# Storing the first tile's output by one transfer of eight rows a partition instead of two of four

## The chip, the cores and the metric

One core of a Trainium2 chip runs the kernel. The metric is the device time of one execution in microseconds (us); a kernel's time is the median of its runs. "Span" is the time from the first to the last instruction in the profiled execution, some 1.3 us less than the device time.

Data moves between HBM (the chip's main memory) and the core's on-chip buffers, which have 128 partitions, by sixteen DMA engines. A load reads HBM, a store writes it. A packet is one data record of the trace: here the rows of one partition in one transfer. A transfer has landed when all engines have reported it (16 updates of its semaphore in the trace). ScalarE computes GELU, VectorE the product, and SyncE only waits and issues transfers.

## The reference

The input has 32 x 512 rows of 2048 float32 values. The first half of each row goes through GELU and is multiplied by the second half:

```
x1, x2 = x[..., :1024], x[..., 1024:]
out = 0.5 * x1 * (1 + erf(x1 / sqrt(2))) * x2
```

So 134.2 MB are read and 67.1 MB written.

## The kernel before

The 16384 rows are cut into 16 tiles of 128 partitions x 8 rows. Tile i uses input buffer i % 2 (64 KB a partition) and output buffer i % 2 (32 KB a partition). SyncE issues all loads and the last three stores (queue q1); ScalarE issues the other stores (queue q10). Tile 0 and tile 15 are computed in three steps, the others in two.

```python
load(0, slice(0, 4), first)
load(0, slice(4, 8), loaded[0])
load(1, slice(0, 8), loaded[1])
...
for i in range(n_tiles):
    k = i % 2
    last = i == n_tiles - 1
    pieces = i == 0 or last
    steps = ((0, 2), (2, 4), (4, 8)) if pieces else ((0, 5), (5, 8))
    if i >= 2:
        nc.scalar.wait_ge(stored[k], n[stored[k].name])   # the output buffer is free
    for lo, hi in steps:
        ...  # ScalarE: GELU of these rows; VectorE: product, counted in mul_done
        if pieces and hi % 4 == 0:
            if last:
                store(nc.sync, i, slice(hi - 4, hi), tail_stored)
            else:
                store(nc.scalar, i, slice(hi - 4, hi), stored[k])
    if not pieces:
        if i == n_tiles - 2:
            store(nc.sync, i, slice(0, R), tail_stored)
        else:
            store(nc.scalar, i, slice(0, R), stored[k])
    if i + 2 < n_tiles:
        nc.sync.wait_ge(mul_done, n[mul_done.name])       # the input buffer is free
        load(i + 2, slice(0, R), loaded[k])
```

Two waits tie the tiles together: tile i's compute needs store i-2 to have landed, and load i+2 is issued only after tile i's compute.

## Time and profile before

| | before |
|---|---|
| median of the runs | 469.6 us (469.56 to 471.63) |
| span of the profiled run | 468.1 us |
| packets of q1 and q10, share of 16 engines' span | 70.5% + 29.1% |
| bytes of HBM over the span | 201.3 MB, 430 GB/s |
| VectorE, ScalarE busy | 30%, 25% |

The lines of the profile, and how they are read, stand in the prediction.

### The profile page before, as it was taken

The page shows a single profiled execution, that of the slowest core. Times are in us where ns is not written, and L with a number is a line of the kernel's source. Part 1 is how long each engine was busy: PE and PEld are TensorE (multiplying, and loading weights), DVE is VectorE, ACT ScalarE, POOL GpSimd, SP SyncE. Part 2 cuts the span into 40 slices and gives each one's busy share as a digit, 9 for nine tenths or more (in the row PEclk, how much of TensorE's full clock was granted, in tenths as well). Part 3 has the DMA queues.
Part 4 walks back from the last instruction along what each step waited for, and adds up shares of the span by engine and source line. Part 5 has one row for each costly group of instructions (what it writes and reads, how often), then busy time and mean ns, then how long its engine had stood idle before and what let it go on. Part 6 is the DMA issues. An engine that isn't in the chain of part 4 may idle for free.

```text
span 468.1 us, 174 instructions
## 1 busy us (share of the span) xinstructions
DVE 140.5 (30%) x34; ACT 115.5 (25%) x35; POOL 0.2 (0%) x4
## 2 busy tenths in 40 slices
DVE  0330514207052060511606116060150702507043
ACT  1320606032060410604106050050500506014060
POOL 0000000000000000000000000000000000000000
DMA  8999899999999999999999999999999999999998
GB/s 358 448 448 442 375 423 496 414 403 445 417 482 403 420 431 493 403 403 448 470 426 403 442 409 493 403 403 448 493 403 403 448 442 454 404 428 423 493 395 367
DMA packets 5041, 201.34 MB, mean 430 GB/s; under 512 B 560, under 2 KB 560, under 8 KB 560
## 3 DMA queue, kind: packets, MB, share of 16 engines
q1 hardware_dynamic: 2880, 142.61, 70.5%
q10 hardware_dynamic: 2160, 58.72, 29.1%
q14 instruction: 1, 0.01, 0.0%
HBM read 134.22 MB, written 67.11 MB: 430 GB/s over the span
## 4 chain that ended last, share of the span: by engine, by line
DMA 76%; DVE 14%; ACT 8%; ACTq 0%; SPq 0%; issue 0%
DMA out_dram<-o_tile 66%; DVE o_tile L87 14%; DMA x_tile<-in_x_dram 10%; ACT o_tile L79 8%; ACTq L110 0%; SPq L47 0%; SPq L63 0%; SPq L58 0%
## 5 line engine op out<-in xcount | busy, mean ns | idle before, releaser
L87 DVE TENSOR_TENSOR o_tile<-o_tile,x_tile 128x5120 f32<-128x5120 f32 (+3 forms) x34 | 140.5, 4170 | 320.2 <-ACT o_tile L79 320.2
L79 ACT ACTIVATE o_tile<-x_tile 128x5120 f32<-128x5120 f32 (+3 forms) x34 | 114.3, 3407 | 337.4 <-DMA out_dram<-o_tile 301.9
L79 ACT ACT_TABLE_LOAD x1 | 1.3, 1283 | 3.3 <-PEq L63 3.3
L133 POOL MEMSET const-bfloat16-1.0<- 128x1 bf16 x1 | 0.1, 102 | 0.0
L133 POOL MEMSET const-uint8-127<- 128x1 uint8 x1 | 0.1, 102 | 0.0
L133 POOL MEMSET const-float32-1.0<- 128x1 f32 x1 | 0.1, 99 | 0.0
L133 POOL MEMSET const-float32-0.0<- 128x1 f32 x1 | 0.1, 98 | 0.2 <-issue 0.2
## 6 DMA issues: line engine op xcount, KB each, us to landing
out_dram<-o_tile ACTq DMA_DIRECT2D x13, 4096.0 KB, 44.7
x_tile<-in_x_dram SPq DMA_DIRECT2D x2, 4096.0 KB, 16.7
out_dram<-o_tile ACTq DMA_DIRECT2D x2, 2048.0 KB, 34.4
out_dram<-o_tile SPq DMA_DIRECT2D x1, 4096.0 KB, 25.1
out_dram<-o_tile SPq DMA_DIRECT2D x2, 2048.0 KB, 7.6
x_tile<-in_x_dram SPq DMA_DIRECT2D x15, 44.5
```

Source lines behind the costliest of these rows:

```text
L79: nc.scalar.activation(out=o_bufs[k][:, rows, :], in_=x_bufs[k][:, rows, :half], func=GELU),
L87: nc.vector.tensor_mul(out=o_bufs[k][:, rows, :], in0=o_bufs[k][:, rows, :], in1=x_bufs[k][:, rows, half:],),
L133: nc = _bacc.Bacc("TRN2", target_bir_lowering=False, num_devices=1)
```

## The change

The intent is fewer, larger transfers: one store of 4 MiB in place of two of 2 MiB. The price is that nothing of tile 0's output can leave before all of tile 0 is computed. Tile 15 keeps its two stores.

```diff
-            if pieces and hi % 4 == 0:
-                if last:
-                    store(nc.sync, i, slice(hi - 4, hi), tail_stored)
-                else:
-                    store(nc.scalar, i, slice(hi - 4, hi), stored[k])
-        if not pieces:
+            if last and hi % 4 == 0:
+                store(nc.sync, i, slice(hi - 4, hi), tail_stored)
+        if not last:
             if i == n_tiles - 2:
                 store(nc.sync, i, slice(0, R), tail_stored)
             else:
```

## The prediction

> **What bounds the kernel now.** I read the page from its head (busy shares, then the DMA row of the slices), then the chain of waits in order of time, then the timeline of the first tiles, and last the windows, cut at the moments that the timeline gave.
>
> ```profile
> span 468.1 us, 174 instructions
> DVE 140.5 (30%) x34; ACT 115.5 (25%) x35; POOL 0.2 (0%) x4
> ...
> DMA  8999899999999999999999999999999999999998
> ...
> DMA packets 5041, 201.34 MB, mean 430 GB/s; under 512 B 560, under 2 KB 560, under 8 KB 560
> q1 hardware_dynamic: 2880, 142.61, 70.5%
> q10 hardware_dynamic: 2160, 58.72, 29.1%
> ```
>
> The two computing engines work under a third of the span. The DMA row is 9 or just below from end to end, and the packets of q1 (SyncE's queue: all loads and the last three stores) and q10 (ScalarE's queue: all other stores) take 70.5 + 29.1 = 99.6% of sixteen engines' span, which is 466.2 of 468.1 us. So the transfers leave about 2 us unfilled in the whole program. The time is their sum, plus the start.
>
> ```profile
> 12.99 3.71 ACT L79 ACTIVATE o_tile<-x_tile 128x2048 f32<-128x2048 f32 x2 [8.43 <-DMA x_tile<-in_x_dram]
> 19.45 0.38 ACTq L53 DMA_DIRECT2D out_dram<-o_tile  x1
> 22.70 3.62 ACT L79 ACTIVATE o_tile<-x_tile 128x4096 f32<-128x4096 f32 x1 [6.00 <-DMA x_tile<-in_x_dram]
> 30.81 0.36 ACTq L53 DMA_DIRECT2D out_dram<-o_tile  x1
> 47.30 7.12 ACT L79 ACTIVATE o_tile<-x_tile 128x5120 f32<-128x5120 f32 x2 [20.99 <-DMA x_tile<-in_x_dram]
> 60.60 0.36 ACTq L53 DMA_DIRECT2D out_dram<-o_tile  x1
> 71.68 7.12 ACT L79 ACTIVATE o_tile<-x_tile 128x5120 f32<-128x5120 f32 x2 [17.25 <-DMA out_dram<-o_tile]
> ...
> 100.68 7.12 ACT L79 ACTIVATE o_tile<-x_tile 128x5120 f32<-128x5120 f32 x2 [21.88 <-DMA out_dram<-o_tile]
> ```
>
> This is the start, from the timeline. Each half of tile 0's load takes 9.7 us (12.99 to 22.70), the first half's store goes out at 19.45, the second's at 30.81. Tile 1 can start at 47.30, tile 2 at 71.68, tile 3 at 100.68, and from there each tile follows 29.0 us after the one before. ScalarE's wait ends with a store's landing, but that is only a name: 8 MiB of load and 4 MiB of store go through in each 29.0 us.
>
> ```profile
> 22.30:46.92 24.62, 4.43 (x1) 3.62 (x1) 0.00 (x0) 1.00 0.99 426
> 46.92:71.60 24.68, 8.76 (x2) 7.12 (x2) 0.00 (x0) 1.00 0.99 428
> 100.68:129.68 29.00, 8.76 (x2) 7.12 (x2) 0.00 (x0) 1.00 1.00 434
> ```
>
> The windows give, in the last two columns, the DMA share and the rate. The two stretches in which tile 0's stores drain (load 1 with the first, load 2 with the second) run at 426 and 428 GB/s, a steady period at 434. That small gap is all that the change can reach in the middle of the stream.
>
> **What the Trainium skill says.** "DMA: Bandwidth & Descriptors", section "Queues, rings and completion order", says each DMA engine goes round-robin between the queues it has work for, one packet at a time. The trace agrees: its packet records alternate between q1 and q10, and a steady period holds, on each engine, eight load packets of 64 KB (2.418 us) and eight store packets of 32 KB (1.213 us): 8 x 3.631 = 29.05 against 29.0 us. The same page, "Where 436 GB/s comes from", puts the ceiling of the sixteen ports at 435.2 GB/s and says that for transfers to or from HBM a lower limit of some 358 binds. The steady 434 shows that here the ceiling, not the lower limit, is what counts. "Perfetto Trace Analysis", section "DMA Optimizations", says splitting may let part of a transfer start sooner, and ties the gain to DMA engines that are generally idle. Here they are not idle, so I expect little loss from undoing the split.
>
> **The change part by part.** Tile 0 still loads in two halves and computes in three steps. Removed: the store issued at 19.45 and that queue entry (0.38 us of ScalarE's sequencer, in a wait of 6.00 us). Added: nothing. Altered: the one store at 30.81 carries eight rows a partition. The order of the other engines' instructions is unchanged.
>
> Packets: tile 0's stores were 16 packets of 16 KB on each engine at 0.611 us = 9.78 us. They become 8 of 32 KB at 1.213 = 9.70 us. Saved: 0.07 us, on the path that sets the end, since the stream is full.
>
> Order: with 16 KB store packets, load 1 and load 2 each took 80% of the bytes while they ran (64 of 80 KB a round). In the changed kernel load 1 runs alone from 22.3 us until the store's first packet. A load issued at 0.94 had its first packet at 1.95, so I take 1.0 us from issue to eligibility: 31.8 us, in the middle of a change of packets. Five load packets then go alone (choosing that the next one is already committed): 22.3 + 5 x 2.42 = 34.4. The other three alternate with 32 KB stores: 3 x 3.63 = 10.9, so load 1's data ends at 45.3; its completion passes behind one more store packet (1.21) and takes 0.4 us as now: tile 1 starts near 46.9 (if only four go alone, 48.1). By then four of store 0's eight packets are out. Load 2 then alternates all along, with the other four of store 0 and then with store 1 (issued at 46.9 + 13.3 = 60.2, in time to follow store 0, which ends near 61.0). Load 2 ends at 45.3 + 8 x 3.63 = 74.3 and tile 2 starts near 75.9, against 71.68 now, 4.2 us later.
>
> That is not lost time: during it three packets of store 1 have gone (3.6 us of stream) which before were still to come. Every later tile keeps the same offset at 29.0 us a tile, with ScalarE released by its load, not by a store. At the end the stores in the ScalarE queue run out three packets before load 15 does, and its last packets go alone. Count the whole stream: from 22.3 us, 15 loads x 8 x 2.418 = 290.2, plus 14 stores x 8 x 1.213 = 135.9, gives 448.4 for the end of the last load, so tile 15 starts at 448.8; before it started at 448.97. The tail is as now: store 14 takes 8 x 1.213 = 9.7, the two halves of the last store 4.9 each, and end of data to landing 0.4: 448.4 + 9.7 + 9.8 + 0.4 = 468.3, which is the span before (468.1) to within the rounding of these terms.
>
> Left over is the rate of the two slow stretches. They hold 40 packets' worth of 32 KB on each engine in 24.62 + 24.68 = 49.3 us; at 29.0/24 = 1.208 us each they would hold it in 48.3. If the changed kernel's stream runs at the steady rate there, it gains 1.0 us (the 0.07 is part of it). The records show single 64 KB packets of 2.5 to 2.8 us there beside 2.418; whether the 16 KB stores cause them or the start of a transfer, the trace does not say, so I take half: 0.5 us. Sum: 469.6 - 0.5 = 469.1 us.
>
> **The rivals.** First, that stores which start 11 us later leave the DMA engines dry. Against it: at 19.45 q1 still holds the rest of load 0 and all 8 MiB of load 1, and the stretch where loads ran alone moved 4 MiB in 9.7 us, 432 GB/s. To lose 2% (9.4 us) the engines would have to stand still for nearly the whole 11 us. It would make 471 to 480.
>
> Second, that the later landing of store 0 becomes a wait for tile 2, which writes the same output buffer. By my count store 0 lands about 62 to 64, load 2 at 75.9, so the wait is covered by 12 us. If it were not, tile 2 would shift, but the next load is already queued and the stream runs on: no change in time.
>
> Third, that the offset of 4.2 us reaches the end: tile 15 starts at 453 instead of 448.8, and its compute up to the last store (448.97 to 460.67 = 11.7 us) is exposed. For it: that is what a fixed period would give. Against it: the stores in ScalarE's queue are finite, and the three packets sent early are missing at the end. It would make 472 to 473.
>
> Fourth, that the slow stretches are fully the small packets' doing: 468.6.
>
> **Range and chances.** 469.1 us; 8 in 10 between 468.3 and 470.4, the upper side for the run-to-run spread (one of three runs before was 471.63) and for a part of the third rival. All rivals but the worst form of the first lie within 2% of 469.6 (460.2 to 479.0). Faster by over 2%: 0.01; within: 0.98; slower: 0.01.
>
> **What would show it.** In the changed profile: DMA packet shares again summing to about 99.6%; tile 1 starting near 47 to 48 and tile 2 near 76 to 77; ScalarE's waits put down to the loads of x_tile instead of stores; stores landing about 34 us after issue instead of 44.7 (issued 13.3 after the tile's start, first packet 18 after, last 47 after); tile 15 starting within half a microsecond of 448.97; the span within 1 us of 468.1. A DMA slice at 7 or less between 19 and 35 us, or tile 15 after 450, would prove me wrong.

## The result, and the profile after

The changed kernel took 470.74 us (median of 6 runs, 470.02 to 471.29) against 469.6 us, a ratio of 1.0016 with a 95% interval of 0.9998 to 1.0035. Ratios here are the mean time of one kernel's fast runs over that of the other's in the same rounds, so not quite the ratio of the medians quoted. Executions over 1.5% slower than the fastest of the same kernel are left out of the means. In a second set of five runs, told below, the ratio was 1.0029 (1.0015 to 1.0043). So there is a small real loss, about a quarter of a per cent, where a small gain was predicted; the median lies 0.3 us above the stated range (the ratio times 469.6 is 470.35, just inside it). The first interval is wide because one of the six runs before took 471.63 us; it has no profile, and none of the 16 later runs of that kernel is above 469.76.

From the page of the changed kernel: the span, the DMA row, and the two queues.

```profile
span 468.7 us, 173 instructions
...
DMA  8998989999999999999999999999999999989998
...
q1 hardware_dynamic: 2880, 142.61, 70.6%
q10 hardware_dynamic: 2016, 58.72, 29.0%
```

The shares sum to 99.6% again, and q10 has 144 records fewer (2160 before): 128 store packets and the 16 completions of the second transfer. Nothing ran dry. Next the timeline of the start (start, duration, engine and line; in brackets how long the engine had been idle and what ended it).

```profile
30.78 0.38 ACTq L53 DMA_DIRECT2D out_dram<-o_tile  x1
46.85 7.12 ACT L79 ACTIVATE o_tile<-x_tile 128x5120 f32<-128x5120 f32 x2 [20.56 <-DMA x_tile<-in_x_dram]
76.00 7.12 ACT L79 ACTIVATE o_tile<-x_tile 128x5120 f32<-128x5120 f32 x2 [22.03 <-DMA x_tile<-in_x_dram]
104.92 7.12 ACT L79 ACTIVATE o_tile<-x_tile 128x5120 f32<-128x5120 f32 x2 [21.80 <-DMA x_tile<-in_x_dram]
...
449.40 7.21 ACT L79 ACTIVATE o_tile<-x_tile 128x2048 f32<-128x2048 f32 x3 [17.98 <-DMA x_tile<-in_x_dram]
```

Tile 1 starts 0.45 us earlier than before, tile 2 then 4.3 us later (76.00 against 71.68), and every further tile keeps that offset until the last, which starts at 449.40 against 448.97. ScalarE is now released by loads where it was released by stores: 337.8 us of its waits are put down to x_tile, none to out_dram. The whole middle of the program has moved by 4 us and the end has not.

The windows show where the stream was not full speed (last column GB/s):

```profile
22.30:45.22 22.92, 4.42 (x1) 3.62 (x1) 0.00 (x0) 1.00 0.95 392
45.20:74.20 29.00, 8.76 (x2) 7.12 (x2) 0.00 (x0) 1.00 1.00 434
```

A window counts a packet whole where it starts, and that misleads here: on most engines load 1's first packet starts just before 22.3 us and is left out, so 392 is too low. With each packet spread over its own time, load 1's stretch ran at 414 GB/s (428 before) and load 2's at 434 (431 before). The packet records of the trace were also taken apart by engine: for each of the 16 DMA engines the chain of its packets (the records name no engine; a packet belongs to the one whose last packet ended at that moment), and by how much single packets exceeded their usual time (2.418 us for 64 KB, 1.213 for 32 KB, 0.611 for 16 KB).

```
packets held up, mean of 16 engines        before      after
first store joins the load stream          0.34 us     1.08 us   (load packets starting 20 to 47 us)
second half store beside load 2            0.11 us     -         (47 to 75 us)
last packet of the slowest engine ends     467.73      468.28 us
```

Before, the excess is spread over several packets of 0.06 to 0.40 us. After, each engine has exactly one, the sixth load packet of load 1 (start near 34 us), which takes 3.43 to 3.59 us instead of 2.42; the first store packet follows it at 37.4 to 38.0 us. More held up: 1.08 - 0.45 = 0.63 us; saved by larger packets: 0.07 us. Together 0.56 us, and the last packet ends 0.55 us later. This accounts for the two profiled spans (468.7 against 468.1), but not for the runs near 471.3.

### The profile page after: what moved, and what is told of

Read it like the earlier page. It is cut to its first block, busy times and chain, and to the rows that moved or that the text cites. A ratio compares the mean times of both kernels' runs of the same rounds, so it can differ in the third digit from the quotient of the medians.

```text
span 468.7 us, 173 instructions
## 1 busy us (share of the span) xinstructions
DVE 140.5 (30%) x34; ACT 115.5 (25%) x35; POOL 0.2 (0%) x4
## 4 chain that ended last, share of the span: by engine, by line
DMA 76%; DVE 14%; ACT 8%; ACTq 0%; issue 0%; SPq 0%
DMA x_tile<-in_x_dram 76%; DVE o_tile L87 14%; ACT o_tile L79 8%; ACTq L107 0%; SPq L47 0%; ACTq L77 0%; SPq L63 0%; SPq L58 0%
## 5 line engine op out<-in xcount | busy, mean ns | idle before, releaser
L79 ACT ACTIVATE o_tile<-x_tile 128x5120 f32<-128x5120 f32 (+3 forms) x34 | 114.3, 3407 | 337.8 <-DMA x_tile<-in_x_dram 337.8
## 6 DMA issues: line engine op xcount, KB each, us to landing
out_dram<-o_tile ACTq DMA_DIRECT2D x14, 4096.0 KB, 33.6
```

What stands on the lines that cost most here:

```text
L79: nc.scalar.activation(out=o_bufs[k][:, rows, :], in_=x_bufs[k][:, rows, :half], func=GELU),
```

## The experiments

Twelve kernels ran, in three groups, each group compared with runs of the kernel before (medians 469.50, 469.50 and 469.57 us).

**Again.** The changed kernel unaltered.

> The changed kernel, unaltered, for a second profile and a tighter interval. Theory of the full stream (the time is the sum of the packets plus what single packets are held up): 470.0 to 471.3 us, the sixth packet of load 1 again held up by about 1.1 us when the first store enters the stream. Rival, that the 1.1 us between the medians is chance: a ratio to the kernel before of 1.000 and a range that covers 469.6.

Measured: 471.32 us (five runs: 470.19, 470.23, 471.32, 471.52, 471.53), ratio 1.0029 (1.0015 to 1.0043). The nine runs of the kernel before beside it lay within 469.41 to 469.58. The sixth packet is held up again, and the rival (chance) falls. The profiled execution was one of the three longer ones, with a span of 470.0 us, and its chains show why:

```
again, engine chains: load packets before the first store, that store's start, packets held up, last end
15 engines    22    37.40 to 37.89 us    0.86 to 1.53 us in all          468.08 to 468.40 us
 1 engine     21    35.13 us             0.80 + 1.83, 2.62 us in all     469.62 us
```

One engine of sixteen took the store one packet earlier than the others and was held up twice. In these records each engine moves eight of a transfer's 128 packets, and a tile starts only after the last engine's (tile 1 at 49.41 us, against 46.85 in the first profile), so this one engine's end sets the time: 469.62 - 468.28 = 1.34 us, and the span is 1.3 us longer than in the first profile. Why an engine takes this turn in some executions is open; the first store's first packet falls close to a change of packets, and the neighbours differ by up to half a microsecond there.

**Two late halves.** Small packets without the early start.

```diff
+            elif i == 0:
+                store(nc.scalar, i, slice(0, 4), stored[k])
+                store(nc.scalar, i, slice(4, 8), stored[k])
```

> Tile 0's output again as two transfers of four rows, but both issued when all of tile 0 is done: small packets without the early start. Full stream with round-robin by packets: 16 packets of 16 KB an engine take 16 rounds beside 64 KB load packets, store 0 lands near 86 us, tile 2 must wait for it, load 4 is issued near 100 instead of 89, and the stream may run dry for 1 to 3 us: about 471.5 us (470 to 473.5). Rival, that only bytes count: 469.6 to 470.7. Rival, that the small packets themselves are the better form: below 469.6.

Measured: 472.11 us, ratio 1.0054 (1.0019 to 1.0088), the four runs at 469.97, 470.37, 473.85 and 473.97. The profiled one was of 470.37: tile 2 starts at 84.04, released by the store (predicted about 86), and the next two tiles close up until the 29 us rhythm is there again. No dry stretch is seen in that execution. What the two runs near 473.9 lose can't be said without a profile of one. In these four runs, small packets without the early start are not better than one large transfer.

**Finer and earlier.** One transfer after each of tile 0's three steps.

```diff
             if last and hi % 4 == 0:
                 store(nc.sync, i, slice(hi - 4, hi), tail_stored)
-        if not last:
+            elif i == 0:
+                store(nc.scalar, i, slice(lo, hi), stored[k])
+        if not pieces:
```

> The other direction: tile 0's output in three transfers, each issued as soon as its step is done (two, two and four rows). Round-robin by packets: 24 store packets an engine instead of 16 or 8, so store 0 needs 24 rounds beside the 64 KB loads and lands near 90 us, although it begins earlier; tile 2 waits for it, load 4 is issued near 103 us, loads and stores in flight are used up near 100 us and the stream is dry for 3 to 5 us: 473 us (471 to 475). Rival, that an earlier start of stores helps or is hidden: 469.6 or less.

Measured: 474.33 us, ratio 1.0102 (1.0088 to 1.0116). The timeline of tiles 1, 2 and 3:

```profile
45.59 7.12 ACT L79 ACTIVATE o_tile<-x_tile 128x5120 f32<-128x5120 f32 x2 [18.20 <-DMA x_tile<-in_x_dram]
88.95 7.12 ACT L79 ACTIVATE o_tile<-x_tile 128x5120 f32<-128x5120 f32 x2 [36.24 <-DMA out_dram<-o_tile]
102.71 7.12 ACT L79 ACTIVATE o_tile<-x_tile 128x5120 f32<-128x5120 f32 x2 [6.63 <-DVE o_tile L87]
```

Tile 2 waits 36 us for store 0, whose first piece went out at 17.36. A window from 98 to 105 us shows what this costs:

```profile
70.00:98.00 28.00, 4.54 (x1) 7.12 (x2) 0.00 (x0) 1.00 0.99 429
98.00:105.00 7.00, 4.22 (x2) 2.29 (x1) 0.00 (x0) 1.00 0.84 286
```

The rate falls to 286 GB/s, and the records have a gap of 2.5 to 3.9 us on every engine before load 4's first packet. The stores began earliest of all kernels, and yet tile 2 was released 4.9 us later than by the 16 packets of the two late halves (84.04), because 24 small packets need 24 turns beside packets of 64 KB. That the turns are counted in packets, not in bytes, is what this run shows.

**Later.** The store of tile 0 only after tile 1.

```diff
-            else:
+            elif i > 0:
+                if i == 1:
+                    store(nc.scalar, 0, slice(0, R), stored[0])
+                store(nc.scalar, i, slice(0, R), stored[k])
```

> More of the change: the one transfer of tile 0 is issued only when tile 1 is done (near 55 us instead of 31). Full stream by my count: loads 1 and 2 run alone to about 58 us, store 0 then needs 8 rounds of 3.63 us and lands near 88 to 90, tile 2 waits for it, load 4 is issued near 103 and the stream is dry for some 5 us: 475 us (472 to 478). Rival, that the order of a stream never matters: 470 to 471. Rival, that each us of a later store costs a us: over 490.

Measured: 474.73 us, ratio 1.0122 (1.0105 to 1.0139). The timeline again:

```profile
42.14 7.12 ACT L79 ACTIVATE o_tile<-x_tile 128x5120 f32<-128x5120 f32 x2 [15.75 <-DMA x_tile<-in_x_dram]
89.18 7.12 ACT L79 ACTIVATE o_tile<-x_tile 128x5120 f32<-128x5120 f32 x2 [39.91 <-DMA out_dram<-o_tile]
102.94 7.12 ACT L79 ACTIVATE o_tile<-x_tile 128x5120 f32<-128x5120 f32 x2 [6.64 <-DVE o_tile L87]
```

Tile 2 waited until 89.18 (expected 88 to 90), and the engines stood still for 2.5 to 3.8 us near 104. (The profiled execution was the slowest of the four, 476.86 us: one engine ended at 475.1, the others at 473.8 to 473.9. The other three lay within 474.65 to 474.74.) Putting the store off by 11 us cost a quarter of a per cent; by 36 us, 1.2%. So both rivals fall: a store's delay is not paid one for one, and the order of the stream does matter once the output buffer comes free after the loads in flight are used up.

**A used queue.** The first of tile 0's rows in each partition is loaded through ScalarE's queue (lines joined in this cut and the next).

```diff
-        load(0, slice(0, 4), first)
+        counted(nc.scalar.dma_start(out=x_bufs[0][:, 0:1, :], in_=x_t[0][:, 0:1, :]), first, 16)
+        load(0, slice(1, 4), first)
```

> The changed kernel, but the first of the four rows of load 0's first half is loaded through ScalarE's queue, so that this queue has been used before the first store. Theory A, that the 1.05 us hold-up of one load packet at the first store is the first use of the second queue: the hold-up goes to under 0.3 us and the time to about 469.8 (469.4 to 470.3). Theory B, that a store packet entering a stream of loads alone holds up the load packet ahead of it by about its own length (1.2 us for 32 KB, 0.6 for 16 KB): hold-up still 0.9 to 1.2 us, 470.0 to 471.5 us, in two groups. Theory C, that issuing store 0 and load 2 within 0.02 us of each other is the cause: as B.

Measured: 470.81 us (470.02 to 471.69), ratio 1.0025 (1.0013 to 1.0038). The packet near 34 us is held up by 0.96 to 1.32 us on fifteen engines; one engine was early again, held up by 0.99 and 1.53 us, in a profiled run of 471.69 us. Theory A, the first use of the queue, falls. The row moved was a load, though: that the first store of a program is special, whatever its queue did before, is not excluded by this run.

**Two issues apart.** An additional VectorE product delays load 2's issue.

```diff
+        if i == 0:
+            counted(nc.vector.tensor_mul(out=o_bufs[1][:, 0:4, :],
+                in0=x_bufs[0][:, 0:4, :half], in1=x_bufs[0][:, 0:4, half:]), mul_done, 1)
+            nc.scalar.wait_ge(mul_done, n[mul_done.name])
```

> The changed kernel, but an additional product on VectorE (4096 elements a partition, 4.4 us, written to the other output buffer before its use and overwritten later) delays the issue of load 2 from 30.8 to about 35.2 us; store 0 is still issued at 30.8, and load 1 runs beyond 41 us, so no supply is lost. Theory C (two issues at once): hold-up of the sixth packet under 0.4 us and about 469.8 us. Theories A (first use of the queue) and B (the store packet's length): hold-up still near 1.05 us, 470.0 to 471.5.

Measured: 470.56 us (469.97 to 471.24), ratio 1.0023 (1.0009 to 1.0036). Load 2 was issued at 35.27, the store at 30.94, and on fifteen of the engines the packet that starts near 34 us was held up by 0.68 to 1.43 us, with a smaller hold-up of the one before on most; the sixteenth again took the store early. So two issues at the same moment are not the cause. But 35.27 still lies inside the held-up packet (34 to 38 us), so this run doesn't exclude that the issue of load 2 plays a part.

**No load in flight, after and before.** Load 1 is issued when tile 0 is done, in each of the two kernels.

```diff
-        load(1, slice(0, 8), loaded[1])
 ...
             nc.sync.wait_ge(mul_done, n[mul_done.name])
+            if i == 0:
+                load(1, slice(0, 8), loaded[1])
```

> The changed kernel without load 1 in flight behind load 0: load 1 is issued only when all of tile 0 is computed. Now the DMA engines are dry from 22.3 us to the first packets after 30.8, about 9.5 us. Full stream: 469.6 + 9.5 = 479 us (477.5 to 481). Rival, that other stages hide it: under 475.

> The kernel before (two stores of four rows) without load 1 in flight, as in the run before this one. The first store, issued at 19.5 us, can now fill 4.9 us of the dry stretch (2 MiB at 16 packets of 0.61 us a half). Full stream: 4.3 to 5 us less than the changed kernel without the load: 474.5 us (473 to 476), a difference of about 1% that the split earns where the engines are dry. Rival, that the split is worth nothing anywhere: no difference.

Measured: 481.90 us with one store (above the expected range) and 476.03 with two (at its upper edge). The split that was worth 1.1 to 1.8 us in the tuned kernel (the differences of the medians in the two sets) is worth 5.9 us here. First the window of the one-store form, then those of the two-store form:

```profile
22.30:31.70 9.40, 4.42 (x1) 3.62 (x1) 0.00 (x0) 1.00 0.00 0
```

```profile
22.30:27.30 5.00, 0.35 (x1) 3.62 (x1) 0.00 (x0) 1.00 0.98 419
27.30:32.30 5.00, 4.08 (x1) 0.00 (x0) 0.00 (x0) 1.00 0.00 0
```

With one store, nothing moves for 9.4 us; with two, the first half moves at 419 GB/s in the first five of these. The expectation counted only the gap: the one-store form lost 12.4 us, not 9.5. The records show the rest as held-up packets: 0.96 to 1.84 us on nearly every engine in the first load packet after the dry stretch, just ahead of the store, smaller ones near 79 us on most, and one engine with 3.7 us in all that ended at 480.6, the others by 479.4. The two-store form also has 0.29 to 1.40 us in that first load packet, so this is not the doing of the one large store alone. The late engine accounts for more than a microsecond of the profiled run: without it the last packets of the two profiled kernels would be 5.1 us apart (479.4 against 474.3), near the 4.3 to 5 us expected.

**The last store's queue, after and before.** Store 14 from ScalarE's queue, in each of the two kernels.

```diff
             if i == n_tiles - 2:
-                store(nc.sync, i, slice(0, R), tail_stored)
+                store(nc.scalar, i, slice(0, R), tail_stored)
```

> The changed kernel with store 14 issued from ScalarE's queue instead of SyncE's. My account of the end says that the offset of some 4 us is given back only because the last stores of ScalarE's queue run out before load 15 does, and store 14 waits behind load 15. Then here store 14 takes every second turn beside load 15's last three packets: load 15 lands 3.6 us or more later, tile 15 starts near 453.5 instead of 449.4 to 450.6, its compute is exposed, and the time is about 473.5 us (472 to 475). Rival, that only the sum of bytes counts: 470 to 471.5.

> The same edit on the kernel before. There load 15 and store 13 end together, so store 14 starts at the same moment on either queue: tile 15 starts at 449 us and the time is unchanged, 469.6 us (469.2 to 470.4). Rival, that the queue of store 14 costs by itself: as much loss as in the changed kernel.

Measured: 473.44 us after the change (ratio 1.0077, 1.0059 to 1.0095), 469.52 us before it (ratio 0.9999, 0.9983 to 1.0015). Tile 15's first line, in the changed kernel with this edit, then in the kernel before with it:

```profile
454.09 7.21 ACT L79 ACTIVATE o_tile<-x_tile 128x2048 f32<-128x2048 f32 x3 [21.52 <-DMA x_tile<-in_x_dram]
```

```profile
449.05 7.21 ACT L79 ACTIVATE o_tile<-x_tile 128x2048 f32<-128x2048 f32 x3 [21.86 <-DMA out_dram<-o_tile]
```

The window in which tile 15 of the former is computed:

```profile
454.00:461.50 7.50, 4.66 (x3) 7.21 (x3) 0.00 (x0) 1.00 0.58 251
```

The offset reaches the end here, tile 15 starts at 454.09, and the stream runs empty under its compute: the records have gaps of 1.7 to 3.5 us on every engine near 461.5. In the kernel before, whose load 15 and store 13 end together, the same edit costs nothing. So the offset of 4 us is real work put off, and what gives it back in the changed kernel is that store 14 queues behind load 15.

**Six rows and two.** Tile 0's output as two transfers of six and two rows, issued together (the edit of the two late halves with other bounds).

> The changed kernel with tile 0's output as two transfers issued together, of six rows (24 KB packets) and two rows (8 KB). Theory B, the hold-up of the load packet at the first store grows with the store packet: between the 0.4 us mean of 16 KB and the 1.05 to 1.3 of 32 KB, about 0.75 to 0.9 us. Rival, a fixed hold-up: 1.0 to 1.3. The time, as with two late halves (16 rounds): 470 to 474.5 us.

Measured: runs at 470.08, 470.11 and 472.72 us, median 470.11 (a fourth, at 479.78, is left out; with it the median is 471.42), ratio 1.0040 (1.0002 to 1.0078). The packet near 34 us is held up by 0.47 to 0.80 us, 0.65 on average. This is between 16 and 32 KB, a little under the range expected.

**Smaller load packets.** Load 1 as two transfers of four rows.

```diff
-        load(1, slice(0, 8), loaded[1])
+        load(1, slice(0, 4), loaded[1])
+        load(1, slice(4, 8), loaded[1])
```

> The changed kernel with load 1 as two transfers of four rows (load packets of 32 KB instead of 64 when the first store arrives). Theory B, the hold-up belongs to the store packet: 1.0 to 1.3 us still. Theory D, it belongs to the load packet: near half, 0.5 to 0.65 us. The time: 469.6 to 471.5 us, since the stream stays full.

Measured: 470.36 us, four runs within 470.19 to 470.45, ratio 1.0017 (1.0001 to 1.0033). The hold-up is spread over two packets, 0.93 us an engine in all, so it is not halved with the load packet, against theory D; it is a little below B's range. Two engines took the store a packet early, but here a packet is 1.2 us, and they ended at 468.4 to 468.5, the others at 467.7 to 468.2. The runs near 471.3 are absent, which fits the account of the early engine, in four runs.

The hold-up at the first store, over the runs (mean an engine, summed over the load packets up to 47 us, of "later" over 50 to 70):

```
store packet   kernel                                  held up
16 KB          before (first store at 19.5 us)         0.34 us (0.21 at the first store, 0.10 at the second)
16 KB          two late halves                         0.94 us (0.41 at the first, 0.49 six us later)
24 KB          six rows and two                        0.70 us (0.65 at the first)
32 KB          after / again                           1.08 / 1.17 us
32 KB          later                                   1.18 us
32 KB          used queue / apart                      1.32 / 1.45 us
```

At the first store it grows with the store packet. Theory B as it was put, that any store packet entering a stream of loads alone holds up a load packet by about its own length, does not hold all the same. In the two kernels without load 1 in flight, store 1 (32 KB packets) also joins loads that have run alone, near 75 to 85 us, and there the load packet ahead of it is held up by only 0.35 us (two stores for tile 0) and 0.30 us (one) on average. What sets the first store apart is not tested. Why a load packet is held up at all when the second queue joins, and why the kernel before pays only half of what the late halves pay for the same packet, stays open. The experiments point to no version that beats the kernel before: what is left in it is under 0.5 us of held-up packets.

## Why the prediction was right or wrong

- **The bound** was right: the packets fill 99.6% of the engines' span in both kernels. The first rival (dry engines) fell for this kernel; taking load 1 out of flight showed what it would have looked like.
- **The order** was right in its numbers: tile 1 at 46.85 (predicted 46.9), tile 2 at 76.00 (75.9), stores landing 33.6 us after issue in the median (34), the waits moved to the loads, tile 15 at 449.40 (448.8). One part was right by compensation: six load packets went alone, not five, and the sixth was held up by 1.08 us. One more load packet and the hold-up, less one pair of 3.63 us, is 2.42 + 1.08 - 3.63 = -0.13 us, so load 1 still ended at 45.2.
- **The second rival** (a wait for store 0) was rightly put aside for this kernel: no wait of ScalarE is put down to a store. Store 0 landed at 64.9 us (predicted 62 to 64), 11 us before tile 2 started. This wait is the one that decided the finer and the later variants, where tile 2 waits to 89 us.
- **The third rival** (the offset reaches the end) was rightly put aside, and for the reason given: moving store 14 to the other queue brings it back, at 473.4 us where the rival was put at 472 to 473.
- **The failed step** is the term "0.5 us gained", from the sentence "If the changed kernel's stream runs at the steady rate there, it gains 1.0 us ... so I take half". Load 2's stretch did rise to 434 GB/s, but load 1's fell from 428 to 414: the held-up packets went from 0.34 + 0.11 to 1.08 us an engine. In place of -0.5 stands +0.63 (with the 0.07 us saved, +0.56), the whole of the profiled difference. I had asked whether small packets or the start of a transfer caused the slow stretches and read it as a loss that the change could only reduce; at the first store the larger packet has the larger hold-up. Why, the runs leave open.
- **A reading behind that step** was wrong too: the 1.0 us of slack. The window of 49.3 us ends at 71.60 us, when load 3 already moves. By the packet records an engine needed 48.8 us on average (22.02 to 70.86) for the 40 packets' worth, against the 48.3 reckoned. So there was about 0.5 us to gain, not 1.0, and the half that was forecast would have been all of it. That the total came within 1.7 us is due to the right account of the full stream, not to this term.
- **A missing term**: the engines can fall out of step. In every profiled execution of the changed start that took 471.2 us or more (again, used queue, apart) one engine had taken the store a packet early; in the one of 470.02 none had. Four profiles agree on this, and no edit tested it. It is about 1.3 us between two executions of one kernel, and the range's upper side did not hold it.

## What to carry to other kernels

Where the packets of all queues sum to the whole span, ask of a merged or split transfer how it changes the turns: in these runs a queue's share of the bytes went by the length of its packets, and a store that gets few bytes a turn lands late and can hold up the buffer that it empties, however early it starts. Check whether the next load is still issued before the ones in flight run out; if it is, the order of the stream is free, and if it isn't, the time is lost. An offset that the middle of a program carries costs only if nothing at the end takes it back, so look at which queue the last transfers stand in.

## What the Trainium skill lacked or had wrong

- "DMA: Bandwidth & Descriptors", section "Queues, rings and completion order": the turn by packets holds, but it gives a packet as some 9 to 17 descriptors, with no length. Here a packet record was a partition's whole contiguous run, 64, 32 or 16 KB, and the share of the bytes followed from that: store 0 took 8 turns of 32 KB, 16 of 16 KB, and in three pieces (8 and 16 KB) 24 turns, landing at about 89 us instead of 65. It also has nothing on a second queue that joins a busy one: at the first store a load packet was held up by 1.08 us (32 KB store packets), 0.65 (24 KB) and 0.2 to 0.4 (16 KB) on average, at a later store of 32 KB packets by 0.30 to 0.35.
- The same page, "Latency and other measured facts", gives some 600 ns to the first byte. The trace agrees for the first load, if one counts from the end of the issuing instruction (1.32 us) to the first packet (1.95): 0.63 us. From the instruction's start it is 1.0 us. The section has nothing on a stream that is full: there the first packet came 5.0 us (before) and 6.6 us (after) after the store's issue, turns and hold-up included.
- The same page, "Where 436 GB/s comes from", says the HBM side of about 358 GB/s binds for transfers to and from HBM. With one core running, 434 GB/s were held over whole tiles. The 358 is given there as half of what two cores share, so the sentence lacks its condition; the fabric's 435 is what fits here.
- "Perfetto Trace Analysis", section "DMA Optimizations", has the condition right (splitting where DMA engines are idle): with load 1 held back, the split earned 5.9 us with the engines dry. It doesn't say that splitting can lose in a full stream: three pieces instead of two cost 1.0%.
